# Input stage of a hybrid attention and convolution layer: meta tokens on ScalarE, position-table products moved to the start

## Chip, core and metric

The kernel runs on one core of a Trainium2 chip. The engines of a core work side by side, each through its own queue in order: TensorE (PE, with its weight loads shown apart as PEld), VectorE (DVE), ScalarE (ACT), GpSimd (POOL) and SyncE (SP), which here only issues loads and stores. ScalarE can issue them too, from its own queue. The metric is the device time of one execution, in microseconds; lower is better.

## The reference, cut to what matters

```python
h = concatenate([meta, x], axis=1)          # 16 meta rows ahead of 1024 rows of x
h = layer_norm(h, in_ln_g, in_ln_b)
z = h @ w_in + b_in                         # q | k | v | convolution input | gates
a = swa_sink_attention(q, k, v, sinks, rel_bias)   # window 128, relative bias by position
...
mixed = sigmoid(g_attn) * (a @ w_attn_proj) + sigmoid(g_conv) * (conv_branch @ w_conv_proj)
h = layer_norm(alpha * h + mixed @ w_out)
f = (gelu(g) * u) @ ffn_w_down              # u, g: up product and 3-tap convolution
return layer_norm(alpha * h + f)[:, 16:]
```

All is float32. The model width is 1024, there are 8 query heads of 64, and the relative bias comes from a table of 32 buckets by 8 heads. The kernel gets a prepared table of 33 rows: 564 columns that say which bucket each distance falls in, and 8 columns with the bias of each bucket. The product of the two parts gives the bias of every distance for every head.

## The kernel before

The layer is one long program, and PE's work through it is dense. The change touches the input stage, the first 25 us or so, and one place at 65 to 77 us.

The rows of x are loaded as eight tiles of 128 rows (`load_x`, L201), the meta rows twice into 32 rows of one tile `xm` (L198), all on SyncE's queue. Each load carries a rank: inside `with rank(p)` the instruction gets priority p, and instructions of a queue are put in the order of their priorities as far as their inputs allow. `load` issues on SyncE, `store` on ScalarE. The first three weight tiles (K, V and the first query tile) are filled with the ranks at L327.

For each group of rows, `stat` (L431) computes mean and variance on VectorE, `table` (L461) the reciprocal root of the variance on ScalarE, `newton` (L466) one Newton step and the shift -mean/std on VectorE in four small instructions, and `norm` (L475) the normed rows in two halves of 512 columns, on VectorE or ScalarE. `turns` (L492) transposes the normed rows on PE in 128-column pieces, `scaled` (L505) applies gain and bias on ScalarE, and `z_first` (L546) makes the first products: for the group of the first 272 rows directly in float32, later with split high and low parts (`high`, `low`, `whigh`, `wlow`). `dv`, `ac` and `pe` tie the instructions of VectorE, ScalarE and PE in this part into one written order each (`in_order`, L413): the list from L574 on is that order.

At its start PE runs 20 products of a constant tile with itself (L575) whose result is not used; each shows as two instructions. At the end of the input part (L663 to L669) stand the two products of the position table (400 and 164 columns, tile `ps_v`), each with a copy to `vrow` on VectorE, and a store of `vrow` to memory (`v1d`). They are tied behind the last first-stage product on PE and the last instruction of the written VectorE order.

Bank tags of PSUM: `mm` has three buffers for the first products, `o` one, `s` and `t` two each.

Of the kernel before, what the change touches and what calls it, by code (L numbers as in the profile page):

```python
# [23 lines left out]
F = mybir.dt.float32  # L24
R = mybir.dt.float32r
AF = mybir.ActivationFunctionType
# [3 lines left out]
P = 128  # L30
D = 1024
KC = D // P
NMETA = 16
# [5 lines left out]
NH = 8  # L39
# [36 lines left out]
RK_TURN, RK_SPLIT, RK_EVAC, RK_START, RK_QKV, RK_RESID, RK_ATT = 450, 500, 600, 1000, 10000, 20000, 30000  # L76
# [3 lines left out]
J_BAND, J_META, J_META0, J_METAQ, J_LEN = 0, 384, 400, 544, 564  # L80
# [32 lines left out]
def tile_hybrid_layer(  # L113
# [3 lines left out]
    nc = tc.nc  # L117
# [5 lines left out]
    def load(o, i):  # L123
        return nc.sync.dma_start(out=o, in_=i)

    def store(o, i):

        return nc.scalar.dma_start(out=o, in_=i)
# [47 lines left out]
    pat = ps_stack.enter_context(tc.tile_pool(name="pat", bufs=1, space=PSUM, reuse_waits="tile"))  # L176
# [3 lines left out]
    start = ExitStack()  # L180
    sp = start.enter_context(tc.tile_pool(name="start", bufs=1, side="right", reuse_waits="tile"))
# [10 lines left out]
    xm = sp.tile([P, D], F, name="xm")  # L192
    with rank(0):
        nc.gpsimd.memset(xm[32:64], 0.0)
        nc.gpsimd.memset(xm[64:96], 0.0)
    with rank(5):
        for i in range(2):
            load(xm[i * NMETA:(i + 1) * NMETA], meta_tokens)  # L198
    xt = []

    def load_x(j):  # L201
# [17 lines left out]

    tab = sp.tile([P, J_LEN + NH], F, name="tab")  # L220
    with rank(0):
        nc.gpsimd.memset(tab, 0.0)
    with rank(25):
        load(tab[:33], table_in)

    def bcol(m):
        return colA[:, m:m + 1]
# [94 lines left out]
    def weights(shape, fill):  # L322
        fills[0] += 1
        n = fills[0]
        own = n == 3
        raw = OB[:, 0:D].rearrange("p (k c) -> p k c", k=KC) if own else wraw(shape)
        with rank({1: 14, 2: 13, 3: 16, 4: 23}.get(n, RK_SPLIT)):  # L327
            last_fill.append(fill(raw))
        hi, lo = chunks(sp.tile([P, W_LEN], R, name="w3") if own else wsp())
        if n <= 3:  # L330
            return hi, lo, raw
        with rank(RK_SPLIT):
            last_split.append(split(raw, hi, lo))
            if n == 7:
                after(last_split[-1], cin_done[-1])
        return hi, lo
# [91 lines left out]
    def src_of(j):  # L428
        return (xt[j], P) if j >= 0 else (xm[:2 * NMETA], 2 * NMETA)

    def stat(t, *js):  # L431

        J = len(tokens[t])
        if t not in norms:
            norms[t] = [sp.tile([P, J, 2], F, name=f"mv{t}")] + [sp.tile([P, J], F, name=f"{n}{t}") for n in "trm"]
        for j in js:
            x_, n = src_of(j)
            st_ = small.tile([P, 2, 6], F, name="st")
            for i in range(2):
                dv(V.bn_stats(st_[:n, i], x_[:, i * 512:(i + 1) * 512]))  # L440
            dv(V.bn_aggr(norms[t][0][:n, tokens[t].index(j)], st_[:n].rearrange("p a b -> p (a b)")))

    def scales():
        dv(V.tensor_scalar(qb, colA[:, 0:4], HD ** -0.5, None, OP.mult))
        dv(V.tensor_scalar(colA[:, 10:30], colA[:, 10:30], 0.5, None, OP.mult))
        dv(V.tensor_scalar(nsink, sink, -1.0, None, OP.mult))

    half_st = {}

    def half_stat(t, j, i):  # L450

# [9 lines left out]
    def table(t):  # L461
        mv, t_, r_, m_ = norms[t]
        n = src_of(tokens[t][0])[1]
        ac(nc.scalar.activation(r_[:n], mv[:n, :, 1], AF.Abs_reciprocal_sqrt, bias=eps[:n], scale=1.0))

    def newton(t):  # L466
        n = src_of(tokens[t][0])[1]
        mv, t_, r_, m_ = (x_[:n] for x_ in norms[t])
        stt = V.scalar_tensor_tensor
        dv(stt(t_, mv[:, :, 1], EPS, r_, OP.add, OP.mult))  # L470
        dv(stt(t_, t_, -0.5, r_, OP.mult, OP.mult))
        dv(stt(r_, t_, 1.5, r_, OP.add, OP.mult))
        dv(stt(m_, mv[:, :, 0], -1.0, r_, OP.mult, OP.mult))

    def norm(t, j, on_dve):  # L475
        x_, n = src_of(j)
        i = tokens[t].index(j)
        mv, t_, r_, m_ = norms[t]
        xns[j] = sp.tile([P, D], F, name="xn", tag="xn", bufs=4) if j >= 0 else xm
        to = xns[j] if j >= 0 else xm[96:]  # L480
        for a in range(0, D, 512):
            if on_dve:
                dv(V.tensor_scalar(to[:, a:a + 512], x_[:, a:a + 512], r_[:n, i:i + 1], m_[:n, i:i + 1], OP.mult, OP.add))
            else:
                ac(nc.scalar.activation(to[:, a:a + 512], x_[:, a:a + 512], AF.Identity, bias=m_[:n, i:i + 1],
                                        scale=r_[:n, i:i + 1]))
        later.append((x_, mv[:n, i, 0:1], r_[:n, i:i + 1], n, j))

    GT = [(-1, 0, 1), (2, 3, 4), (5, 6, 7)]
    turned, tms = {}, {}  # L490
# [1 line left out]
    def turns(g, *ks):  # L492
        n = len(GT[g])
        c = HG[g][1] - HG[g][0]
        at = {}
        for k in ks:
            at[k] = pat.tile([P, 512], F, name="ps_h0", tag="st"[k % 2], bufs=2)
            turned[g, k] = at[k][:, n * P - c:n * P]
        for tiles in (GT[g][:2], GT[g][2:]):
            for k in ks:  # L500
                for j in tiles:
                    i = GT[g].index(j)
                    pe(nc.tensor.transpose(at[k][:, i * P:(i + 1) * P], xns[j][:, k * P:(k + 1) * P], ident))
# [29 lines left out]
    def whigh(i):  # L533
        ac(nc.scalar.copy(first[i][0], first[i][2]))
# [36 lines left out]

    tc.cur_priority = RK_START
    warm = pat.tile([P, 512], F, name="ps_w", tag="o")
    for i in range(20):  # L574
        pe(nc.tensor.matmul(warm[:, :P], ones, ones, start=True, stop=True))  # L575
    stat(0, -1)
    table(0)
    stat(1, 0)
    newton(0)
    norm(0, -1, False)  # L580
    stat(1, 1)
    table(1)
    newton(1)
    norm(1, 0, True)
    norm(1, 1, False)
    scales()
    turns(0, 0, 1, 2, 3)
    stat(2, 2)
    scaled(0, 0)
# [8 lines left out]
    evac(0, 0)  # L598
    stat(2, 3)
    stat(2, 4)  # L600
    whigh(1)
    table(2)
    z_first(0, (1,), *range(8), raw=True)
    evac(0, 1)
    newton(2)
# [55 lines left out]
    first_nm = dv_done[-1]  # L661

    tc.cur_priority = RK_RESID + 1000  # L663
    vrow = sp.tile([P, J_LEN + 104], F, name="vrow")[:NH, :J_LEN]
    for a, b in ((0, 400), (400, J_LEN)):
        ps = pat.tile([P, 512], F, name="ps_v", tag="o" if a == 0 else "t", bufs=1 if a == 0 else 2)
        after(nc.tensor.matmul(ps[:NH, :b - a], tab[:, J_LEN:], tab[:, a:b], start=True, stop=True), pe_done[-1])
        after(nc.vector.tensor_copy(vrow[:, a:b], ps[:NH, :b - a]), first_nm)
    load(v1d, vrow)  # L669

    tc.cur_priority = RK_QKV + 3000
# [1176 lines left out]
```

## Time and profile before

| | us |
|---|---|
| three runs | 1264.09, 1262.23, 1264.21 (median 1264.09) |
| the profiled execution, its own time | 1263.24 |
| its span in the trace | 1261.5 |

A row of a view names start and duration, engine, line, operation, the tile written and the tiles read, and in brackets the idle time before it and what ended it. PE's busy time counts overlapping instructions once; a full column of it does not say that each product ran at its fastest.

### The profile page before, as it was taken

Reading aid. Unit: us, or ns where it says so; the run is one execution under the profiler, and the core shown is the slowest. Engines: PE = TensorE matmul, PEld = TensorE weight load, DVE = VectorE, ACT = ScalarE, POOL = GpSimd, SP = SyncE. Lnnn points to the kernel's source line nnn. Section 1 sums busy time; section 2 is a strip of 40 time slices with the busy share of each in tenths; the row PEclk is TensorE's granted clock in tenths of the full one; section 3 lists DMA queues with packets and bytes.
Section 4 is the critical chain, followed back from the end, with each engine's and each line's share of the span. In section 5 each row is a group of like instructions: output and inputs, shape, how many; then the busy total and the mean of one; then the engine's idle time right before and its main releaser. Section 6 shows DMA issues by size and latency. Waiting matters only on the chain.

```text
span 1261.5 us, 23038 instructions
## 1 busy us (share of the span) xinstructions
PE 1247.8 (99%) x9186; PEld 1181.3 (94%) x9186; DVE 1076.5 (85%) x1858; ACT 595.0 (47%) x1100; POOL 8.0 (1%) x9
## 2 busy tenths in 40 slices
PE   8999999999999999999999999999999999999997
PEld 7999999999999999788999999999999998888886
DVE  7888999999978677448999999998989977996697
ACT  7532345655474233335665555554455544445330
POOL 0000000001000000000000000000000000000000
PEclk9999999999999999999999999999999999999999
DMA  6375543332256564222245546453454567998712
GB/s 254 105 256 145 170 120 97 106 93 85 72 155 169 164 166 124 84 85 82 68 157 196 196 171 216 160 209 135 157 205 165 192 225 252 392 353 329 271 63 84
DMA packets 98701, 212.19 MB, mean 168 GB/s; under 512 B 11411, under 2 KB 38611, under 8 KB 98338
## 3 DMA queue, kind: packets, MB, share of 16 engines
q1 hardware_dynamic: 84474, 199.64, 47.3%
q10 hardware_dynamic: 14120, 11.08, 2.8%
q8 instruction: 72, 1.18, 0.4%
q14 instruction: 35, 0.29, 0.1%
HBM read 150.29 MB, written 62.70 MB: 169 GB/s over the span
## 4 chain that ended last, share of the span: by engine, by line
PE 96%; DVE 2%; ACT 1%; DMA 0%; issue 0%; SPq 0%; DVEq 0%; ACTq 0%
PE px L1549 15%; PE py L1549 10%; PE ps_x L1694 9%; PE ps_z L342 8%; PE ps_z L345 8%; PE ps_z L346 8%; PE ps_z L1694 7%; PE pw L1549 5%; PE pz L1549 5%; PE ps_p L346 2%; PE ps_p L345 2%; PE ps_p L342 2%; PE ps_w L346 2%; PE ps_w L342 2%; PE ps_w L345 2%; PE ps_z L560 2%
## 5 line engine op out<-in xcount | busy, mean ns | idle before, releaser
L342 PE MATMUL ps_z<-RHO,w 128*128 128x256 f32 (+2 forms) x864 | 243.4, 282 | 0.0
L345 PE MATMUL ps_z<-RHO,w 128*128 128x256 f32 (+2 forms) x864 | 242.2, 280 | 0.0
L346 PE MATMUL ps_z<-RHC,w 128*128 128x256 f32 (+2 forms) x864 | 242.2, 280 | 0.0
L342 PEld LDWEIGHTS ps_z<-RHO,w 128*128 128x128 f32 x864 | 162.5, 188 | 1.2 <-ACT FA L709 0.7
L345 PEld LDWEIGHTS ps_z<-RHO,w 128*128 128x128 f32 x864 | 162.5, 188 | 0.5
L346 PEld LDWEIGHTS ps_z<-RHC,w 128*128 128x128 f32 x864 | 162.7, 188 | 0.2
L729 DVE SCALAR_TENSOR_TENSOR FA<-cin,cdw,FA 128x1026 f32<-128x1026 f32 x120 | 154.4, 1297 | 0.7
L1371 DVE TENSOR_TENSOR RHO<-wr,RHO 128x512 fp32r<-128x512 f32 x94 | 64.2, 691 | 7.9 <-ACT RHO L1370 7.9
L304 ACT CAST w<-wr 128x1024 fp32r<-128x1024 f32 x37 | 38.8, 1048 | 63.9 <-PE ps_z L346 45.0
L1370 ACT CAST RHO<-wr 128x512 fp32r<-128x512 f32 x94 | 56.8, 620 | 24.0 <-DVE wr L1388 11.8
L1388 DVE TENSOR_TENSOR wr<-wr 128x512 f32<-128x512 f32 x88 | 60.9, 692 | 0.1
L738 ACT ACTIVATE FA<-ps_z,colr 128x258 f32<-128x258 f32 (+1 forms) x64 | 30.1, 472 | 59.8 <-PE ps_z L346 48.9
L307 DVE TENSOR_TENSOR w<-wr,w 128x1024 fp32r<-128x1024 f32 x37 | 45.1, 1218 | 9.6 <-ACT w L304 9.4
L1561 ACT COPY FA<-px 128x514 f32<-128x514 f32 (+2 forms) x23 | 13.2, 573 | 76.8 <-PE px L1549 76.8
L1371 DVE TENSOR_TENSOR w<-wr,w 128x512 fp32r<-128x512 f32 x60 | 40.9, 691 | 4.8 <-ACT w L1370 4.7
L1549 PE MATMUL px<-OA,RHO 128*128 128x258 f32 x324 | 43.2, 282 | 0.0
L1476 ACT ACTIVATE FA<-OB,coll 128x512 f32<-128x512 f32 x44 | 35.9, 816 | 14.9 <-DVE OB L1557 14.9
L1370 ACT CAST w<-wr 128x512 fp32r<-128x512 f32 x60 | 36.3, 618 | 12.7 <-DMA wr<-in_w_up_dram 5.7
L1561 ACT COPY OB<-px 128x514 f32<-128x514 f32 (+2 forms) x46 | 26.1, 568 | 33.1 <-PE px L1549 33.0
L1549 PE MATMUL px<-OC,RHO 128*128 128x256 f32 x324 | 41.5, 277 | 0.0
L1549 PE MATMUL px<-RHC,RHO 128*128 128x258 f32 (+1 forms) x312 | 41.1, 281 | 0.0
L1549 PEld LDWEIGHTS px<-OA,RHO 128*128 128x128 f32 x324 | 40.5, 189 | 0.2 <-ACT OB L1561 0.2
(451 smaller groups left out, 3302.7 us busy)
## 6 DMA issues: line engine op xcount, KB each, us to landing
wr<-in_w_up_dram SPq DMA_DIRECT2D x44, 512.0 KB, 3.6
wr<-in_w_z_dram SPq DMA_DIRECT2D x29, 512.0 KB, 4.3
OB<-in_w_down_dram SPq DMA_DIRECT2D x24, 512.0 KB, 4.9
fd<-FA SPq DMA_DIRECT2D x44, 256.0 KB, 2.0
FA<-sd SPq DMA_DIRECT2D x15, 512.0 KB, 8.7
qt<-qd SPq DMA_DIRECT2D x28, 256.0 KB, 4.5
OB<-td SPq DMA_DIRECT2D x14, 512.0 KB, 10.0
sgd<-FA ACTq DMA_DIRECT2D x48, 128.0 KB, 3.0
```

Of the source, the lines that this page charges most:

```text
L304: ins = nc.scalar.copy(hi, raw)
L307: return nc.vector.tensor_tensor(lo, raw, f32(hi), OP.subtract)
L342: ins = nc.tensor.matmul(ps, al, bh, start=i == 0, stop=False)
L345: nc.tensor.matmul(ps, ah, bh, start=False, stop=False)
L346: last = nc.tensor.matmul(ps, ah, bl, start=False, stop=i == n - 1)
L729: nc.vector.scalar_tensor_tensor(acc[c], cin[:, j:j + U], wc, acc[c], OP.mult, OP.add)
L1370: nc.scalar.copy(hi, src)
L1371: ins = nc.vector.tensor_tensor(lo, src, f32(hi), OP.subtract)
L1388: ins = nc.vector.tensor_tensor(*x)
L1549: ins = nc.tensor.matmul(o, x[:, ks], bmat(sub, q, hl, k), start=first and k + j == 0, stop=k == 3 and j == 2, skip_group_check=not first)
L1561: copied.append(nc.scalar.copy(*x))
L1694: nc.tensor.matmul(banks[i], l[:, ts], r[:, ws], start=first and a and x + k == 0, stop=z and x == len(ops) - 1 and k == 2, skip_group_che ...
```

## The change

- The meta rows are loaded by ScalarE's queue with rank -1, ahead of all else there.
- The position table is cleared by VectorE instead of GpSimd, and loaded by ScalarE's queue with rank 1 instead of SyncE's with rank 25.
- The first three weight tiles have ranks 13, 16 and 19 instead of 14, 13 and 16.
- The idle products are 16 instead of 20, and both products of the table follow them directly on PE. The 164-column one takes an `mm` bank and is copied to `vrow` behind `scales()`; the 400-column one keeps the `o` bank until its copy at the old place.
- The Newton step of the meta rows runs on ScalarE, in seven small instructions (`newton_act`), and their norm is cut into its two halves, the second behind the reciprocal root of x0 and x1.
- The reciprocal root of the second group stands before, not behind, the split of the second weight tile.

```diff
-    with rank(5):
+    with rank(-1):
         for i in range(2):
-            load(xm[i * NMETA:(i + 1) * NMETA], meta_tokens)
+            store(xm[i * NMETA:(i + 1) * NMETA], meta_tokens)
...
     with rank(0):
-        nc.gpsimd.memset(tab, 0.0)
-    with rank(25):
-        load(tab[:33], table_in)
+        nc.vector.memset(tab, 0.0)
+    with rank(1):
+        store(tab[:33], table_in)
...
-        with rank({1: 14, 2: 13, 3: 16, 4: 23}.get(n, RK_SPLIT)):
+        with rank({1: 13, 2: 16, 3: 19, 4: 23}.get(n, RK_SPLIT)):
...
+    c15 = sp.tile([P, 1], F, name="c15")
+    nc.vector.memset(c15, 1.5)
...
+    def newton_act(t):
+        n = src_of(tokens[t][0])[1]
+        mv, t_, r_, m_ = (x_[:n] for x_ in norms[t])
+        act = lambda *x, **y: ac(nc.scalar.activation(*x, AF.Identity, **y))
+        act(m_, mv[:, :, 0], scale=-1.0)
+        act(t_, mv[:, :, 1], bias=eps[:n], scale=1.0)
+        for i in range(2):
+            act(t_, t_, scale=r_)
+        act(t_, t_, bias=c15[:n], scale=-0.5)
+        act(t_, t_, scale=r_)
+        act(m_, m_, scale=t_)
+        norms[t][1:3] = norms[t][2:0:-1]
...
-    for i in range(20):
+    for i in range(16):
         pe(nc.tensor.matmul(warm[:, :P], ones, ones, start=True, stop=True))
+    ps_v = []
+    vrow = sp.tile([P, J_LEN + 104], F, name="vrow")[:NH, :J_LEN]
+    for a, b in ((0, 400), (400, J_LEN)):
+        ps = pat.tile([P, 512], F, name="ps_v", tag="o" if a == 0 else "mm", bufs=1 if a == 0 else 3)
+        pe(nc.tensor.matmul(ps[:NH, :b - a], tab[:, J_LEN:], tab[:, a:b], start=True, stop=True))
+        ps_v.append((a, b, ps))
     stat(0, -1)
     table(0)
+    newton_act(0)
+    norm(0, -1, False, (0,))
     stat(1, 0)
-    newton(0)
-    norm(0, -1, False)
     stat(1, 1)
     table(1)
+    norm(0, -1, False, (512,))
     newton(1)
     norm(1, 0, True)
     norm(1, 1, False)
     scales()
+    dv(V.tensor_copy(vrow[:, 400:], ps_v[1][2][:NH, :J_LEN - 400]))
     turns(0, 0, 1, 2, 3)
...
+    table(2)
     whigh(1)
-    table(2)
...
-    vrow = sp.tile([P, J_LEN + 104], F, name="vrow")[:NH, :J_LEN]
-    for a, b in ((0, 400), (400, J_LEN)):
-        ps = pat.tile([P, 512], F, name="ps_v", tag="o" if a == 0 else "t", bufs=1 if a == 0 else 2)
-        after(nc.tensor.matmul(ps[:NH, :b - a], tab[:, J_LEN:], tab[:, a:b], start=True, stop=True), pe_done[-1])
-        after(nc.vector.tensor_copy(vrow[:, a:b], ps[:NH, :b - a]), first_nm)
+    after(nc.vector.tensor_copy(vrow[:, 0:400], ps_v[0][2][:NH, :400]), first_nm)
     load(v1d, vrow)
```

More of the change, by code (lines that the diff above doesn't have):

```diff
@@ L473, in newton, with norm @@
         dv(stt(m_, mv[:, :, 0], -1.0, r_, OP.mult, OP.mult))
-    def norm(t, j, on_dve):
+    def newton_act(t):
[10 more added lines that the diff above has]
+        norms[t][1:3] = norms[t][2:0:-1]
+    def norm(t, j, on_dve, halves=(0, 512)):
         x_, n = src_of(j)
@@ L478, in norm @@
         mv, t_, r_, m_ = norms[t]
-        xns[j] = sp.tile([P, D], F, name="xn", tag="xn", bufs=4) if j >= 0 else xm
+        if halves[0] == 0:
+            xns[j] = sp.tile([P, D], F, name="xn", tag="xn", bufs=4) if j >= 0 else xm
         to = xns[j] if j >= 0 else xm[96:]
-        for a in range(0, D, 512):
+        for a in halves:
             if on_dve:
@@ L486, in norm @@
                                         scale=r_[:n, i:i + 1]))
-        later.append((x_, mv[:n, i, 0:1], r_[:n, i:i + 1], n, j))
+        if halves[-1]:
+            later.append((x_, mv[:n, i, 0:1], r_[:n, i:i + 1], n, j))
     GT = [(-1, 0, 1), (2, 3, 4), (5, 6, 7)]
```

## The prediction

> **What bounds the kernel now.** I read the page first: the engines' totals and the chain that ended last, then the busy time by stretches.
>
> ```profile
> span 1261.5 us, 23038 instructions
> PE 1247.8 (99%) x9186; PEld 1181.3 (94%) x9186; DVE 1076.5 (85%) x1858; ACT 595.0 (47%) x1100; POOL 8.0 (1%) x9
> PE 96%; DVE 2%; ACT 1%; DMA 0%; issue 0%; SPq 0%; DVEq 0%; ACTq 0%
> 17.10:160.00 142.90, 142.65 (x1134) 139.61 (x1132) 128.47 (x192) 61.13 (x116) 0.00 (x0) 1.00 0.57 170
> 160.00:340.00 180.00, 179.67 (x1466) 176.10 (x1465) 177.30 (x377) 97.31 (x263) 5.29 (x2) 1.00 0.34 93
> ```
>
> TensorE sets the end. The columns of the last two rows are the stretch, its length, then the busy time of PE, PEld, DVE, ACT and POOL, the granted clock, the DMA share and GB/s. From 17.10 us on PE has no pause worth naming (0.25 us in 143), so whatever brings that point forward, and whatever PE no longer executes after it, comes off the end. One reserve against this: between 160 and 340 us VectorE is busy 177.3 of 180 us, so it could bind there as well.
>
> The profiled execution took 1263.24 us, 1.74 more than its span; the sum below starts from it. It lies 0.85 under the median of the shown runs, 1264.09.
>
> **The input stage, as the order of events.** The next view is the timeline of all engines, start and duration in us.
>
> ```profile
> 0.73 1.28 ACT L187 ACT_TABLE_LOAD   x1 [0.73 <-PEq L1837]
> 0.74 0.86 SPq L124 DMA_DIRECT2D xm<-in_meta_tokens_dram  x2
> 1.08 6.58 PE L575 MATMUL ps_w<-ones 128*128 128x128 f32 x40 [1.08 <-DVE ones L241]
> 1.64 0.90 SPq L124 DMA_DIRECT2D x<-in_x_dram  x2
> 1.73 0.57 POOL L222 MEMSET tab<- 128x572 f32 x1
> 2.03 0.20 ACT L187 ACTIVATE nsink<-eps 128x1 f32<-128x1 f32 x1
> 3.45 1.27 DVE L440 BATCH_NORM_STATS2 st<-xm 32x6 f32<-32x512 f32 x2 [2.41 <-DMA xm<-in_meta_tokens_dram]
> 4.99 0.29 ACT L464 ACTIVATE r<-mv,eps 32x1 f32<-32x1 f32 x1 [2.76 <-DVE mv L441]
> 5.40 1.29 DVE L440 BATCH_NORM_STATS2 st<-x 128x6 f32<-128x512 f32 x2 [0.44 <-DMA x<-in_x_dram]
> 7.42 1.27 DVE L440 BATCH_NORM_STATS2 st<-x 128x6 f32<-128x512 f32 x2
> 7.53 1.51 ACT L485 ACTIVATE xm<-xm,m,r 32x512 f32<-32x512 f32 x2 [2.25 <-DVE m L473]
> 8.72 0.21 DVE L441 BATCH_NORM_AGGREGATE mv<-st 128x2 f32<-128x12 f32 x1
> 9.07 0.29 ACT L464 ACTIVATE r<-mv,eps 128x2 f32<-128x2 f32 x1
> 10.18 1.00 DVE L483 TENSOR_SCALAR xn<-x,r,m 128x512 f32<-128x512 f32 x2
> 10.78 0.33 PE L503 MATMUL ps_h<-coll,xn 128*128 128x128 f32 x1 [2.04 <-DVE xn L483]
> ```
>
> PE's real work waits for a chain on VectorE: statistics of the meta rows (taken up by ScalarE at 4.99), of x0 (from 5.40, after 0.44 us of waiting for its load), the meta rows' Newton step, then x1 (7.42 to 8.93), reciprocal root, Newton, norm, and the transposes at 10.78. x1 takes 1.51 us of VectorE; x0 to x1 is 7.42 - 5.40 = 2.02, so the meta Newton step stands in the chain with 0.51.
>
> **Loads and Newton step.** Two things leave the chain. The two meta loads leave SyncE's queue, so x0 is issued at 0.74 instead of 1.64, 0.90 earlier; every later load moves up too. ScalarE issues them at the same 0.74, ahead of its table load, so the meta statistics keep 3.45. If x0 lands 0.9 earlier, at about 4.5, it is there before VectorE is done with the meta rows, and the 0.44 goes. The Newton step goes to ScalarE: the 0.51 goes. Together 0.95.
>
> ScalarE pays seven small instructions. Bounds from rows: 0.20 (nsink) to 0.29 (the root) each, 1.4 to 2.0 us. From 5.28 they end at 6.7 to 7.3, and the first half of the meta norm (1.51 / 2) at 7.4 to 8.1. The root for x0 and x1 is wanted at 8.93 + 0.14 - 0.95 = 8.12, so they are just covered; the second half norm stands behind that root, beside VectorE's Newton step. Were this cover gone, everything over 8.1 would be paid one to one. Ends: 0.95 if all holds, -0.3 if the table load (1.28) came ahead of the meta loads (VectorE then 1.28 late, less the 0.95). I take **0.9**, since each margin is positive but thin. The transposes then start at about 9.88.
>
> The Trainium skill, "DMA: Bandwidth & Descriptors", section "Issuing engines are not separate DMA queues", speaks against more: loads of several engines share 16 DMA engines, and a second issuer saves only issue time. That is the 0.90 us of the SyncE row; if bytes and not issue time set x0's landing, the sum would lose the 0.44 at most.
>
> The clear of the table moves from GpSimd (0.57) to VectorE ahead of the ones tile: PE starts its idle products at about 1.66 instead of 1.08. 32 instead of 40 instructions at the mean 6.58 / 40 = 0.165 last 5.3 us, to 6.9; both table products (1.14, below) end near 8.1, before 9.88. One vrow copy moves into VectorE's pause before x2; SyncE's moved weights (ranks 13, 16, 19) trade places with x2 to x4, which now come earlier; the weights they pass are used only after 17 us. These I cost at nothing; a weight over 2 us late would show as a PE pause there.
>
> **The clock.** The busy time by stretches that match the clock's steps (same columns as above), and PE's timeline.
>
> ```profile
> 8.40:11.81 3.41, 1.33 (x10) 1.17 (x11) 2.38 (x11) 2.46 (x4) 0.00 (x0) 1.00 1.02 412
> 11.81:15.22 3.41, 3.32 (x12) 2.23 (x11) 2.84 (x7) 2.57 (x5) 0.00 (x0) 0.50 1.02 416
> 612.56:615.97 3.41, 2.43 (x21) 2.42 (x21) 2.43 (x5) 3.41 (x9) 0.00 (x0) 1.00 0.82 222
> 615.97:619.39 3.42, 3.42 (x30) 3.30 (x28) 3.38 (x6) 3.42 (x8) 0.00 (x0) 1.00 0.44 144
> 12.54 1.27 PE L557 MATMUL ps_z<-FA,wr 128*128 128x272 f32 x2
> 14.25 1.11 PE L557 MATMUL ps_z<-FA,wr 128*128 128x272 f32 x2
> 15.53 0.62 PE L557 MATMUL ps_z<-FA,wr 128*128 128x272 f32 x2
> 16.31 0.62 PE L557 MATMUL ps_z<-FA,wr 128*128 128x272 f32 x2
> ```
>
> PE was busy 1.33 of 3.41 us (39%), and in the next 3.41 us the granted clock was 0.50. At 612.56 a stretch with 2.43 (71%) was followed by no drop. The price: the rounds of transposes and first products begin at 12.54, 14.25, 15.53, 16.31 and 17.10; at half clock a round takes 1.71 and 1.28, at full clock 0.78. Four at 0.785 are 3.14 instead of 4.56: **1.42** if the drop goes, 0 if it stays. With transposes 0.9 earlier the same stretch holds 1.33 + 0.9 = 2.23 (65%), or 1.93 (57%) if the lone meta transpose falls before it. Both are nearer to 71% than to 39%, so I take 1.42, with doubt.
>
> The Trainium skill, "TensorE: Matmul & The Clock Gate", section "What's actually happening", lets the clock fall after an idle window of about 3.4 us, in windows that run freely. Here it fell with no pause over 2.04 us in the rows, so the trace disagrees with that strict reading; by it the term would be 0. Free-running windows would let the term change from run to run.
>
> **The table products.** PE's timeline where they stood:
>
> ```profile
> 64.87 0.28 PE L345 MATMUL ps_z<-RHO,w 128*128 128x256 f32 x1
> 64.98 0.28 PE L346 MATMUL ps_z<-RHC,w 128*128 128x256 f32 x1
> 65.19 0.84 PE L667 MATMUL ps_v<-tab 128*8 128x400 f32 x2
> 65.96 0.38 PE L342 MATMUL ps_z<-RHO,w 128*128 128x256 f32 x1
> ...
> 71.69 0.29 PE L346 MATMUL ps_z<-RHC,w 128*128 128x272 f32 x1
> 71.91 0.44 PE L667 MATMUL ps_v<-tab 128*8 128x164 f32 x2
> 72.28 0.39 PE L342 MATMUL ps_z<-RHO,w 128*128 128x256 f32 x1
> ```
>
> Start to start they hold PE 0.77 and 0.37, 1.14 together, in a stretch without a pause. From the product before to the one behind it is 0.98 and 0.59, where an ordinary step is 0.11 and 0.13: 0.87 + 0.46 = **1.33** with the changeover. At the start they stand where PE waits for VectorE anyway, so they cost nothing there if the table has landed.
>
> **Sum:** 0.9 + 1.42 + 1.33 = 3.65; 1263.24 - 3.65 = 1259.6 us.
>
> **The rivals.**
>
> *The clock falls all the same* (chance 0.20). For it: the boundary between 39% and 71% is not known, and the idle products end only a little later than before. Then 2.23 is left: 1261.0.
>
> *The gain is lost between 160 and 340 us* (0.17). For it: VectorE is 98.5% busy there, and the order of instructions is set at build time for all engines. If its work there begins at the same time whatever PE does, the 3.65 turns into PE pauses: about 1263.2, no change. Against: VectorE has 14 us of pauses before 160 (142.90 - 128.47), so its dense stretch begins when PE delivers.
>
> *The table comes late* (0.18). PE takes its queue in order, so every transpose waits behind the table products. The load is issued by ScalarE after two meta issues (0.86), the table load (1.28) and nsink (0.20), at about 3.2. The DMA issues show what landing can take; the columns are count, KB each and median us to landing:
>
> ```profile
> xm<-in_meta_tokens_dram SPq DMA_DIRECT2D x2, 64.0 KB, 2.2
> x<-in_x_dram SPq DMA_DIRECT2D x8, 512.0 KB, 9.0
> kd<-FA ACTq DMA_DIRECT2D x1, 136.0 KB, 2.3
> ```
>
> If it goes like the last ACT row, it lands at 5.5, in time. If it shares the fate of the x loads (9.0), it lands at 12.2; PE has then paused since 6.9, the products run at half clock (2.3), and the transposes start at 14.5 instead of 10.78, 3.7 late. With the four rounds slow as before and 1.33 saved later, that is 2.4 slower: 1265.6; at 11 us to landing 1267.6. It decides from a landing 6.8 us after issue: 3.2 + 6.8 + 2.3 = 12.3 is 10.78 plus the 1.33 saved, rounded up. Against it: the table is 33 rows of 572 numbers (75 KB) on a queue with nothing but the meta loads before it.
>
> **How the numbers follow.** The forecast has 0.45, the others as given. 0.2% is 2.5 us, about what a measurement of this kernel can tell from no change. Against 1264.09 the forecast and the clock rival lie beyond it (under 1261.56): 0.65, less 0.05 for a forecast that falls short by a few tenths: faster 0.60. The lost gain (0.17), that share and the mild end of a late table (0.03) are 0.25 for same. The rest of the late table, 0.15, is slower. The ends of the chain and product terms (0.95 and 1.33, -0.3 and 1.14) put the forecast alone between 1259.5 and 1261.0. Below that the range goes to 1258.0, since the fastest run before, 1262.23, is 1.0 under the profiled one and the changeover may cost a few tenths more than its rows show. With the rivals it runs to 1265.0, which leaves out the worse part of the late table.
>
> **What would show it.** Right: x0's statistics directly behind the meta rows' at about 4.98; transposes of x0 near 9.9; no half-clock stretch before 20 us and rounds of 0.78 throughout; the 24 products that began at 17.10 begin near 14.8; no table product at 65 and 72. Wrong: PE waiting for the table's load; ScalarE reaching the second root after 8.3; a half-clock stretch behind the transposes; or a start that is 2 us ahead at 17 us and level again at 340.

## The result and the profile after

| | median us | lowest to highest | ratio to before, 95% interval |
|---|---|---|---|
| kernel before, the 9 runs beside it | 1263.02 | 1262.09 to 1264.21 | |
| changed kernel, 9 runs | 1266.64 | 1265.96 to 1267.48 | 1.0030 [1.0021, 1.0038] |

The forecast was 1259.6. The changed kernel is 3.6 us slower, and the highest time of the range, 1265.0, is 1.6 under it. The profiled execution took 1266.68 us. From its page, the engines' totals and the chain that ended last:

```profile
span 1264.7 us, 23024 instructions
PE 1248.0 (99%) x9178; PEld 1182.3 (93%) x9178; DVE 1074.4 (85%) x1856; ACT 596.4 (47%) x1107; POOL 7.4 (1%) x8
PE 88%; DVE 7%; DMA 2%; ACT 1%; issue 1%; DVEq 0%; ACTq 0%; SPq 0%
```

PE has eight instructions less and the same busy time; in the chain, VectorE went from 2% to 7% and loads from 0% to 2%. The timeline of the start:

```profile
0.75 0.89 ACTq L128 DMA_DIRECT2D xm<-in_meta_tokens_dram  x2
0.75 0.86 SPq L124 DMA_DIRECT2D x<-in_x_dram  x2
6.75 1.27 DVE L440 BATCH_NORM_STATS2 st<-xm 32x6 f32<-32x512 f32 x2 [5.09 <-DMA xm<-in_meta_tokens_dram]
8.18 1.22 DVE L440 BATCH_NORM_STATS2 st<-x 128x6 f32<-128x512 f32 x2
8.26 1.12 PE L597 MATMUL ps_v<-tab 128*8 128x400 f32 x4
8.49 0.18 ACT L480 ACTIVATE m<-mv 32x1 f32<-32x1 f32 x1
9.56 1.23 DVE L440 BATCH_NORM_STATS2 st<-x 128x6 f32<-128x512 f32 x2
10.20 0.29 ACT L480 ACTIVATE m<-m,t 32x1 f32<-32x1 f32 x1
10.52 0.81 ACT L501 ACTIVATE xm<-xm,m,t 32x512 f32<-32x512 f32 x1
10.83 0.21 DVE L441 BATCH_NORM_AGGREGATE mv<-st 128x2 f32<-128x12 f32 x1
11.36 0.30 ACT L466 ACTIVATE r<-mv,eps 128x2 f32<-128x2 f32 x1
13.07 0.33 PE L520 MATMUL ps_h<-coll,xn 128*128 128x128 f32 x1 [1.34 <-DVE xn L499]
14.83 1.27 PE L574 MATMUL ps_z<-FA,wr 128*128 128x272 f32 x2
16.54 1.11 PE L574 MATMUL ps_z<-FA,wr 128*128 128x272 f32 x2
```

Both queues issue at 0.75, as forecast. The meta statistics, though, wait 5.09 us for the load and begin at 6.75 instead of 3.45. The x0 statistics follow at 8.18 without a wait and x1 ends at 10.83 + 0.21 = 11.04. The first transpose of x0 is at 13.07 instead of 10.78, 2.29 late. The table's products, at 8.26, delay nothing. The busy time by stretches (start and end; length; busy time of PE, PEld, DVE, ACT, POOL; granted clock, DMA share, GB/s), the first three cut where the record of the granted clock, which goes in steps of 3.41 us, cuts them in this execution:

```profile
7.33:10.74 3.41, 1.99 (x12) 0.96 (x10) 3.34 (x8) 2.26 (x9) 0.00 (x0) 1.00 1.03 411
10.74:14.15 3.41, 1.38 (x11) 1.22 (x12) 2.58 (x13) 3.22 (x5) 0.00 (x0) 1.00 1.03 411
14.15:17.57 3.42, 3.28 (x12) 2.20 (x10) 3.32 (x9) 2.56 (x5) 0.00 (x0) 0.50 1.02 407
77.00:100.00 23.00, 22.72 (x192) 22.52 (x191) 17.91 (x22) 5.98 (x10) 0.00 (x0) 1.00 0.88 272
100.00:160.00 60.00, 59.06 (x522) 58.78 (x521) 55.56 (x79) 19.54 (x40) 0.00 (x0) 1.00 0.55 141
```

The last two stretches in the kernel before:

```profile
77.00:100.00 23.00, 23.00 (x200) 23.00 (x199) 18.87 (x22) 5.98 (x10) 0.00 (x0) 1.00 0.79 235
100.00:160.00 60.00, 59.87 (x532) 59.67 (x530) 55.49 (x83) 20.03 (x41) 0.00 (x0) 1.00 0.56 152
```

The clock falls to 0.50 here too, at 14.15 instead of 11.81, and again behind a stretch in which PE was busy for only 40% (1.38 of 3.41). PE stands still for 0.28 + 0.94 us between 77 and 160, where it stood still for 0.13 in all before.

For where the time went, the two traces are laid side by side: the offset is the start of an instruction in one kernel less the start of the same instruction (n-th with the same operation, tiles and shape) in the kernel before, in the two profiled executions. For PE, changed kernel against before:

```
at us     11    17    64    74    90   340   606   609   end
offset +2.29 +2.31 +2.06 +0.50 +1.40 +2.62 +2.60 +3.60 +3.23
```

It begins 2.29 late, wins 1.56 where the table's products no longer run (64 to 74), loses 2.12 by 340 and another 1.00 at 607. The spans differ by the last column; 0.2 more lies outside them.

### The profile page after: what moved, and what is told of

It is laid out like the page before. It is cut to its first block, busy times and chain, and to the rows that moved or that the text cites. A ratio compares the mean times of both kernels' runs of the same rounds, so it can differ in the third digit from the quotient of the medians.

```text
span 1264.7 us, 23024 instructions
## 1 busy us (share of the span) xinstructions
PE 1248.0 (99%) x9178; PEld 1182.3 (93%) x9178; DVE 1074.4 (85%) x1856; ACT 596.4 (47%) x1107; POOL 7.4 (1%) x8
## 4 chain that ended last, share of the span: by engine, by line
PE 88%; DVE 7%; DMA 2%; ACT 1%; issue 1%; DVEq 0%; ACTq 0%; SPq 0%
PE px L1570 15%; PE py L1570 10%; PE ps_x L1715 9%; PE ps_z L1715 7%; PE ps_z L342 6%; PE ps_z L345 6%; PE ps_z L346 6%; PE pz L1570 5%; PE pw L1570 5%; DVE FA L750 3%; PE ps_p L345 2%; PE ps_p L346 2%; PE ps_p L342 2%; PE ps_w L346 2%; PE ps_w L342 2%; PE ps_w L345 2%
```

## Experiments

All times are medians, each with its ratio to runs of the kernel before on the same chip beside it.

| run | median us | ratio, 95% interval | offset at 17 | 64 | 74 | 340 | 606 | 609 | end |
|---|---|---|---|---|---|---|---|---|---|
| e1_meta_sp | 1261.86 | 0.9993 [0.9984, 1.0001] | -1.66 | -1.91 | -3.48 | -2.14 | -2.14 | -1.14 | -1.50 |
| e2_meta_act_alone | 1266.24 | 1.0024 [1.0015, 1.0034] | +2.62 | +2.32 | +2.32 | +2.24 | +2.23 | +2.23 | +2.07 |
| e3_products_alone | 1262.33 | 0.9996 [0.9987, 1.0005] | -1.15 | -1.48 | -3.05 | -2.08 | -2.09 | -1.04 | -1.28 |
| e4_products_late | 1266.78 | 1.0030 [1.0018, 1.0042] | +3.80 | +3.46 | +3.47 | +4.39 | +3.53 | +3.53 | +3.78 |
| e5_one_meta_load | 1268.55 | 1.0046 [1.0032, 1.0060] | +5.27 | +5.03 | +3.47 | +4.09 | +4.09 | +5.07 | +4.80 |
| e6_newton_dve | 1266.42 | 1.0027 [1.0016, 1.0038] | +3.35 | +3.19 | +1.62 | +2.63 | +2.63 | +3.61 | +3.26 |
| e8_bank_t | 1261.87 | 0.9993 [0.9984, 1.0002] | -1.38 | -1.73 | -3.30 | -2.71 | -2.71 | -2.72 | -2.82 |
| e9_no_products | 1262.53 | 0.9997 [0.9988, 1.0006] | -1.11 | -1.14 | -2.71 | -2.51 | -2.53 | -2.53 | -2.60 |
| e10_split_meta | 1261.75 | 0.9993 [0.9984, 1.0002] | -1.28 | -1.73 | -3.30 | -2.31 | -2.30 | -2.30 | -2.42 |
| e11_bank_alone | 1264.33 | 1.0012 [1.0003, 1.0020] | -0.11 | +1.93 | +1.21 | +1.22 | +1.21 | +1.21 | +1.06 |
| e12_pause_filled | 1263.85 | 1.0005 [0.9996, 1.0014] | -1.20 | -1.02 | -1.02 | -1.40 | -1.41 | -1.41 | +0.00 |
| e13_bank_t_fill | 1261.70 | 0.9992 [0.9984, 1.0001] | -0.19 | -0.53 | -2.09 | -1.52 | -1.53 | -1.53 | -1.52 |
| e14_after_bank_t | 1266.47 | 1.0028 [1.0018, 1.0039] | +3.53 | +3.18 | +1.61 | +3.50 | +3.50 | +3.50 | +3.90 |
| e15_order_before | 1266.02 | 1.0027 [1.0017, 1.0036] | +2.21 | +1.97 | +0.40 | +1.35 | +1.51 | +2.55 | +2.33 |
| e16_order_before_bank_t | 1265.93 | 1.0026 [1.0015, 1.0037] | +2.64 | +2.41 | +0.84 | +1.52 | +1.52 | +1.52 | +2.08 |

The offsets come from one execution each, the medians from 4 to 11, so the two can differ by about 1 us.

### The meta loads (e1, e2, e10, e5)

**Back on SyncE, in the changed kernel:**

```diff
-    with rank(-1):
+    with rank(5):
         for i in range(2):
-            store(xm[i * NMETA:(i + 1) * NMETA], meta_tokens)
+            load(xm[i * NMETA:(i + 1) * NMETA], meta_tokens)
```

> The changed kernel with the two meta loads back on SyncE's queue, rank 5, all else as changed. Theory Q (loads are served in the order of issue over both queues: the second meta load stood behind x0 and x1, and VectorE waited for it until 6.75 us): meta statistics start near 3.5, those of x0 near 5.4, first transpose of x0 near 10.3 instead of 13.07, time 1262 to 1263. Theory S (ScalarE's seven small instructions and the table's load are what is late): first transpose of x0 not before 11, time 1264 or more.

Its timeline:

```profile
0.75 0.86 SPq L124 DMA_DIRECT2D xm<-in_meta_tokens_dram  x2
3.44 1.27 DVE L440 BATCH_NORM_STATS2 st<-xm 32x6 f32<-32x512 f32 x2 [1.78 <-DMA xm<-in_meta_tokens_dram]
5.76 1.29 DVE L440 BATCH_NORM_STATS2 st<-x 128x6 f32<-128x512 f32 x2 [0.81 <-DMA x<-in_x_dram]
7.20 1.23 DVE L440 BATCH_NORM_STATS2 st<-x 128x6 f32<-128x512 f32 x2
12.19 0.72 PE L574 MATMUL ps_z<-FA,wr 128*128 128x272 f32 x2 [0.34 <-ACT FA L526]
13.08 0.62 PE L574 MATMUL ps_z<-FA,wr 128*128 128x272 f32 x2
```

This one part undone takes 4.8 us off the median. The meta rows are there at 3.44 again. x0 to x1 is 7.20 - 5.76 = 1.44 instead of 2.02, so the Newton step is out of VectorE's chain, as forecast; x0 itself waits 0.81 instead of 0.44, with the table's load now beside it.

**Alone on ScalarE, in the kernel before** (the same four lines the other way round):

> The kernel before with only the two meta loads moved to ScalarE's queue, rank -1. Theory Q: meta statistics start after 6 us, first transpose of x0 near 13.5, time 1266 to 1267. Theory S: meta statistics start near 3.5, time within 1 us of before (1263).

```profile
0.74 0.89 ACTq L128 DMA_DIRECT2D xm<-in_meta_tokens_dram  x2
6.68 1.28 DVE L440 BATCH_NORM_STATS2 st<-xm 32x6 f32<-32x512 f32 x2 [5.64 <-DMA xm<-in_meta_tokens_dram]
8.12 1.22 DVE L440 BATCH_NORM_STATS2 st<-x 128x6 f32<-128x512 f32 x2
```

Nothing but the queue of two loads of 64 KB is edited; SyncE then issues x0 and x1 0.9 earlier. PE executes the same instructions in the same order as before, and VectorE all but one, at 220 us. The meta statistics begin at 6.68, and the kernel is 3.1 us slower (1266.24 beside 1263.10): this move by itself is most of the 3.6 of the whole change. The parts don't simply add up. With the meta loads on SyncE the rest of the change is worth about -1.2 (e1, not told from no change), with them on ScalarE nothing that can be told (1266.64 beside 1266.24).

**One on each queue,** in e8 (below):

```diff
+    with rank(-1):
+        store(xm[0:NMETA], meta_tokens)
     with rank(5):
-        for i in range(2):
-            load(xm[i * NMETA:(i + 1) * NMETA], meta_tokens)
+        load(xm[NMETA:2 * NMETA], meta_tokens)
```

> The kernel with the 164-column product in a bank of t (1261.87 in an earlier run), with one of the two meta loads issued by ScalarE ahead of all else, the other by SyncE as before; x0 is then SyncE's second load instead of its third. Theory Q (a load lands in the order of its issue among all loads, and the second meta load was late only because x0 and x1 were issued between): both meta loads are issued ahead of x0, so the meta statistics start at 3.4 to 3.8 and x0's at 5.0 to 5.4, the first transpose of x0 at 9.9 to 10.3. Rival S (a load on ScalarE's queue is late by itself beside SyncE's): the meta load on ScalarE lands at 4.8 as the first one did in the changed kernel, the meta statistics start there, the first transpose at 11.1 to 11.6; time 1 above, 1262.8.

```profile
0.75 0.43 ACTq L128 DMA_DIRECT2D xm<-in_meta_tokens_dram  x1
0.75 0.39 SPq L124 DMA_DIRECT2D xm<-in_meta_tokens_dram  x1
1.20 0.88 SPq L124 DMA_DIRECT2D x<-in_x_dram  x2
3.42 1.27 DVE L441 BATCH_NORM_STATS2 st<-xm 32x6 f32<-32x512 f32 x2 [1.76 <-DMA xm<-in_meta_tokens_dram]
4.85 1.28 DVE L441 BATCH_NORM_STATS2 st<-x 128x6 f32<-128x512 f32 x2
7.17 1.29 DVE L441 BATCH_NORM_STATS2 st<-x 128x6 f32<-128x512 f32 x2 [0.79 <-DMA x<-in_x_dram]
```

ScalarE's load of 64 KB is there by 3.42: its queue is not slow in itself. In the changed kernel the other load issued at 0.75 was x0 with 512 KB, and the second meta load came beside x1. By the trace they landed at 4.76 and 6.65, x0 between them at 5.86; here, with both small loads issued ahead of all large ones, they are there by 3.03 and 3.39. x0 no longer waits (4.85), and now x1 does, 0.79, so the first transpose comes no sooner than in e1: offset -0.33, in e1 -0.36. When a load lands thus hangs on what was issued ahead of it or at the same moment, on either queue. Theory Q's strict order of issue goes too far: in the changed kernel nothing was issued ahead of the first meta load, and it still landed 1.4 later than here. That agrees with the Trainium skill, "DMA: Bandwidth & Descriptors", section "Issuing engines are not separate DMA queues": loads of all engines run on the same 16 DMA engines and interleave.

**Both copies in one load of ScalarE, in the changed kernel:**

```diff
-        for i in range(2):
-            store(xm[i * NMETA:(i + 1) * NMETA], meta_tokens)
+        store(xm[:2 * NMETA], dram(meta_tokens, 0, [[0, 2], [D, NMETA], [1, D]]))
```

> The changed kernel with both copies of the meta rows in one load of 128 KB, still on ScalarE's queue at 0.75. Theory Q (loads of both queues are served in the order of issue, and the second meta load stood behind x0 and x1 because it was issued after them; it landed at 6.64): the one load is issued before x1 and partly before x0, so the meta statistics start between 4.8 (the landing of the first meta load) and 5.9 (that of x0), 0.9 to 2.0 ahead of 6.75, and the first transpose of x0 stands at 11.1 to 12.2 instead of 13.07. Time 0.5 to 2 us under the changed kernel (1264.6 to 1266.1 beside 1266.6). Rival S (ScalarE's queue is slow in itself, whatever is issued when): the statistics stay at 6.75 and the time at 1266.6.

Neither: it was the slowest of all. The timeline, and the busy time of two stretches:

```profile
9.46 1.27 DVE L439 BATCH_NORM_STATS2 st<-xm 32x6 f32<-32x512 f32 x2 [7.80 <-DMA xm<-in_meta_tokens_dram]
8.00:9.00 1.00, 0.00 (x0) 0.00 (x0) 0.00 (x0) 0.00 (x0) 0.00 (x0) 1.00 0.98 298
9.00:10.00 1.00, 0.16 (x1) 0.12 (x2) 0.54 (x1) 0.00 (x0) 0.00 (x0) 1.00 0.37 141
```

The load's packets of 4 KB run in the trace as two trains, 0.16 us from packet to packet at first, from 3.57 on, then between the packets of x and the weights until past 8; from 9 to 10 the DMA share is down to 0.37. Two trains fit a load that went to two of the 16 engines. The Trainium skill states such a rule, "DMA: Bandwidth & Descriptors", section "Why a DMA increments its semaphore by 16 and not by 1": the number of engines is the largest up to 16 that divides the outermost sizes of both patterns, and here one of them is 2. The kernel says nothing about order of issue; it tested another thing than was meant.

### The Newton step (e6)

```diff
-    newton_act(0)
-    norm(0, -1, False, (0,))
     stat(1, 0)
+    newton(0)
+    norm(0, -1, False, (0,))
```

> The changed kernel with the meta rows' Newton step back on VectorE, at its old place between x0 and x1. The prediction's theory (the step on ScalarE takes 0.51 off the chain): x1's statistics start 0.5 later, transposes at 13.5, time 0.5 above the changed kernel, 1267.1. Rival N (ScalarE's seven instructions, 2.0 us in the trace, hold up the root for x0 and x1 by as much as VectorE saves): the root stands 0.2 to 0.5 later than 11.36, the transposes at 13.1 to 13.4, time within 0.3 of the changed kernel, 1266.4 to 1266.9.

x1's statistics end later than in the changed kernel and ScalarE is free at once, but its root for x0 and x1 comes at 11.58 instead of 11.36 and the transposes at 13.29 instead of 13.07: 0.22, inside what the rival gave. Counted from the x0 statistics, which began 0.11 earlier in e6 (8.07 against 8.18), it is 0.33, so the move keeps 0.33 of its 0.51. ScalarE's seven instructions run from 8.49 to 10.49 in the changed kernel, 2.00 us, the upper of the bounds taken for them; with the half norm behind them (10.52 to 11.33) they hold the root, due at 11.04 + 0.14 = 11.18, until 11.36. That is the missing 0.18. The time (1266.42) can't be told from the changed kernel's, and e6 has its instructions in another order from about 120 us on.

### The products of the table (e3, e4, e9)

**The table's part alone** in the kernel before, with the change's products and copies:

```diff
-        nc.gpsimd.memset(tab, 0.0)
-    with rank(25):
-        load(tab[:33], table_in)
+        nc.vector.memset(tab, 0.0)
+    with rank(1):
+        store(tab[:33], table_in)
...
-    for i in range(20):
+    for i in range(16):
...
```

> The kernel before with only the table's part of the change: cleared by VectorE, loaded by ScalarE's queue with rank 1, 16 idle products and both table products behind them, one vrow copy early. If PE sets the end at 65 to 150 us, the removed products are worth 1.3 to 1.7 us: 1261.3 to 1261.7. If VectorE sets it there (theory V: from 17 us on VectorE works without pause, and what PE saves turns into waits for cin and for the attention blocks), 0 to 0.9 us: 1262.1 to 1263.

**Products and copies at their old place** in the changed kernel:

```diff
-    ps_v = []
...
-        ps_v.append((a, b, ps))
...
+        after(nc.tensor.matmul(ps[:NH, :b - a], tab[:, J_LEN:], tab[:, a:b], start=True, stop=True), pe_done[-1])
+        after(nc.vector.tensor_copy(vrow[:, a:b], ps[:NH, :b - a]), first_nm)
```

> The changed kernel with the two table products and both vrow copies back at their old place (the table's early load stays). Theory V: VectorE sets the pace, only its copy counts: 1266.6 to 1267.5. If PE sets it: 1.3 to 1.7 us slower than the changed kernel, 1268 or more.

**No products** in the kernel before (the relative bias is then not computed):

```diff
-        ps = pat.tile([P, 512], F, name="ps_v", tag="o" if a == 0 else "t", bufs=1 if a == 0 else 2)
-        after(nc.tensor.matmul(ps[:NH, :b - a], tab[:, J_LEN:], tab[:, a:b], start=True, stop=True), pe_done[-1])
-        after(nc.vector.tensor_copy(vrow[:, a:b], ps[:NH, :b - a]), first_nm)
+        after(nc.vector.tensor_copy(vrow[:, a:b], tab[:NH, a:b]), first_nm)
```

> The kernel before, with both products of the position table left out and the two copies to vrow reading the table's own rows instead, so the relative bias is not computed. All else is as before, the start too. The prediction's theory (PE has no pause from 17 us on, so what it no longer executes at 65 and 72 us comes off the end): 1.33 less at the end, 1261.7 beside 1263.0. Rival V (VectorE sets the pace from 50 to 340 us): PE is 1.2 to 1.7 ahead at 78 us, gives it back as pauses before VectorE's results by 160 us, and the end is within 0.4 of the kernel before, 1262.6 to 1263.0.

In every kernel without them at 65 and 72 us PE wins 1.56 or 1.57 between 64 and 74 us. By 90 us 0.5 to 0.9 of it is given back (0.48 in e9, 0.90 in the changed kernel). A part of that is a pause at one row, here that of e9 and then that of the changed kernel, where PE waits for VectorE to finish a tile; the rest does not show as a pause:

```profile
75.49 0.39 PE L342 MATMUL ps_z<-RHO,w 128*128 128x256 f32 x1 [0.19 <-DVE cin L715]
```

```profile
78.79 0.38 PE L342 MATMUL ps_z<-RHO,w 128*128 128x256 f32 x1 [0.28 <-DVE cin L738]
```

From 17 to 606 us e9 wins 2.53 - 1.11 = 1.42 in the trace, near the 1.33 of the forecast. Its median is only 0.5 lower, with an interval that takes in no change, and lies nearer to rival V's forecast. How much of the 1.42 reaches the time is therefore open. e3's median, 1262.33, lies where theory V had put it: its trace wins 1.57 by 74, loses 0.97 of it by 340 and another 1.05 at 607 (see below). e4's, 1266.78, does too, but e4 against the changed kernel is no pure test: its clock fell for longer (+3.80 at 17, against +2.31), and its instructions stand in another order, see below.

### The granted clock (e12, e13)

24 idle products instead of 20 in the kernel before (e12), and 18 instead of 16 in e8 (e13):

```diff
-    for i in range(20):
+    for i in range(24):
```

> The kernel before with 24 idle products instead of 20, so that PE's pause ahead of the transposes at 10.78 starts at 9.0 to 10.2 instead of 7.7; nothing else. The prediction's clock term (with PE busy for more of that stretch the granted clock does not fall, worth 1.42): rounds of 0.78 throughout, the 24 products at 17.10 start 1.1 to 1.4 earlier, the time 0.4 to 1.1 under the kernel before (of whose runs about a third have the higher mean clock already), 1262.0 to 1262.6. Rival: the fall does not hang on this pause: rounds of 1.71 and 1.28 as before, 1263.0.

> The kernel with the 164-column product in a bank of t and the meta loads on SyncE's queue (1261.87), with 18 idle products instead of 16, so that the table's products end at about 9.9, just ahead of the transposes at 10.34. If the clock falls in some executions because of the pause of 0.9 that is left there: a higher mean clock in all runs and 1261.4. If two more products delay the transposes, or the fall does not hang on this pause: 1261.9 to 1262.3.

Two stretches of the profiled execution of e12, then two of e13, each cut where the clock's record cuts them in that execution (to 0.04 us):

```profile
6.80:10.20 3.40, 2.71 (x24) 2.47 (x23) 2.66 (x12) 1.81 (x3) 0.00 (x0) 1.00 0.99 370
10.20:13.60 3.40, 2.37 (x17) 2.01 (x18) 2.67 (x9) 3.10 (x6) 0.00 (x0) 1.00 1.03 419
```

```profile
8.15:11.56 3.41, 1.86 (x13) 1.15 (x12) 2.87 (x13) 2.62 (x4) 0.00 (x0) 1.00 1.02 399
11.56:14.98 3.42, 3.39 (x12) 2.35 (x11) 3.07 (x9) 2.56 (x5) 0.00 (x0) 0.50 1.03 418
```

PE busy for 80% of the first stretch: no fall, and the first 17 us are 1.20 shorter. At 55% (1.86 of 3.41) it fell, and most of that is lost again (-0.19 at 17). Over all the traces of this case a fall followed the stretches with 9 to 40% and two with 47 and 55%, and none followed any with 58% or more at full clock; three with 43 to 46% went by without a fall, so the busy time of PE alone does not draw the line. The fall lasted one stretch of 3.41 us where PE was busy for 96% or more of it, and two where it was 33 to 90% (e4, e5, e6, e14, e16); in e4 and e14 the offset grows by 1.2 between 11 and 17. The idle products lasted only 5.72 us in this execution of e13, and up to 6.51 (changed kernel) where there are four fewer instructions, so a fixed number does not fill the pause each time.

The fall comes and goes between executions of one kernel. The traces have one execution of each, but they tell how to read the runs: all six without a fall have a mean granted clock of 0.998 or more, all eleven with one 0.997 or less. Of 33 runs of the kernel before, 22 had a mean granted clock of 0.997 or less and took 1263.32 on average, 11 had 0.998 or more and took 1261.98. In the other three sets of its runs beside the experiments the difference is 0.85, 1.26 and 1.36, and of all 100 runs 35 had the higher clock. With the table's products in the pause and the meta rows in time, 37 of 55 runs had 0.998 or more (e1, e3, e8, e10, e13); of the changed kernel's nine, none. The lower time forecast for e12 did not come: it has the higher clock in 7 of 11 runs, and loses what it won between 800 and 1100 us (offset -1.11 to +0.01), with its instructions in another order; whether that order is the cause was not tested. e13's median, 1261.70, with the higher clock in 6 of 11 runs, is neither of its two forecasts.

### The loss at 607 us, and the order of the program (e8, e11, e14 to e16)

In the changed kernel and then in e1, the first product of the up stage waits for VectorE to empty a bank:

```profile
610.67 1.53 PE L1570 MATMUL px<-OC,RHO 128*128 128x256 f32 x11 [0.79 <-DVE OB L1325]
```

```profile
605.93 1.65 PE L1570 MATMUL px<-OC,RHO 128*128 128x256 f32 x12 [0.78 <-DVE OB L1325]
```

The 164-column product had moved from a bank of `t` to one of `mm`, which turns the rotation of three banks by one. e8 is e1 with the bank of `t`; PE and VectorE keep the order of e1:

```diff
-        ps = pat.tile([P, 512], F, name="ps_v", tag="o" if a == 0 else "mm", bufs=1 if a == 0 else 3)
+        ps = pat.tile([P, 512], F, name="ps_v", tag="o" if a == 0 else "t", bufs=1 if a == 0 else 2)
```

> The changed kernel with the meta loads back on SyncE's queue (1261.86 in an earlier run), and the 164-column product in a bank of t, as before, instead of one of mm. Theory B (one more tile in mm shifts the rotation of its three banks, so that at 607 us the up stage's first products get a bank that VectorE has not emptied yet, which costs 0.9): the offset against the kernel before stays at -2.1 from 600 to the end instead of shrinking to -1.3, and the time is 0.7 to 1.0 lower, about 1261.0, ratio 0.9985. Rival: the loss at 607 comes from the earlier arrival at that stage and not from the bank: the time stays at 1261.9.

The offset stays where it was at 606 (-2.71 to -2.72), where e1 lost 1.00. The medians, 1261.86 and 1261.87, don't show it: the time came out as the rival had it. The other way round, the bank alone changed in the kernel before:

> The kernel before, at its old place the 164-column product takes a bank of mm instead of t; nothing else. Theory B (the shifted rotation of mm costs about 0.9 at 607 us): the offset to the kernel before is 0 up to 600 and +0.9 to +1.0 from 609 on, the time 0.8 to 1.0 higher, 1263.9. Rival: the loss at 607 comes with an earlier start alone: no offset, 1263.0.

It did more than that. The two products now stand at 56 us, and 1.2 us are lost by 74; and PE's instructions from about 120 us on stand in another order. A planner orders the whole program at build time, so one edit can move instructions far from it. In the traces PE keeps the order of the kernel before, but for the products at the start and those of the table, in e1, e2, e3, e5, e8, e9 and e13 (in e10 one instruction is moved as well). The changed kernel has another order from about 120 us on, and e11 has, from 90 us on, the changed kernel's on PE and VectorE; e4, e6 and e12 have others. On VectorE the changed kernel's order leaves the old one at the taps of the convolution, about 96 us. The changed kernel with 14 idle products in place of 16 has the order of the kernel before. So e14 is the changed kernel with the bank of `t`, as in the diff of e8, in its own order; e15 is the changed kernel with this one line, and e16 has both edits:

```diff
-    for i in range(16):
+    for i in range(14):
```

> The changed kernel with the 164-column product in a bank of t instead of one of mm; the order of the instructions on PE and VectorE is that of the changed kernel. Theory B (the bank costs about 1.0 at 607 us): the offset to the kernel before stays where it is at 606 us instead of rising by 1.0, and the time is 0.7 to 1.0 under the changed kernel, 1265.7. Rival: the loss at 607 is only moved on and the end stays, 1266.6.

> The changed kernel with 14 idle products instead of 16. With 14, the planner that orders the program at build time puts the instructions of PE and VectorE behind the input stage (from about 105 us on) in the order of the kernel before; with 16 it puts them in another (2225 lines of difference on PE instead of 102). Theory O (that other order is where the saving of the table's products went between 90 and 600 us): the first transpose stays near 13.1, the offset is +2.3 at 17, +0.5 at 74, +1.0 to +1.4 at 90 and no more than that up to 600, the time 1 to 1.5 under the changed kernel, 1265.1 to 1265.6. Rival V (VectorE, which starts 2.2 later than before, sets the pace there): the offset climbs to +2.1 to +2.6 by 340 all the same, time 1266.2 to 1266.6.

> The changed kernel with both: 14 idle products (order of the kernel before) and the 164-column product in a bank of t. Theories O and B together: 1264.2 to 1264.8, so that only the late start (2.3 us) less the products' saving is left. Rivals V and no bank effect: 1266.2 to 1266.6.

From e15, two stretches to hold against those of the changed kernel:

```profile
77.00:100.00 23.00, 22.71 (x195) 22.51 (x194) 17.90 (x22) 5.98 (x10) 0.00 (x0) 1.00 0.90 270
100.00:160.00 60.00, 59.64 (x528) 59.43 (x528) 56.46 (x82) 19.74 (x41) 0.00 (x0) 1.00 0.54 146
```

Up to 100 us both stand still alike (0.28 and 0.29). From 100 to 160 PE is idle 0.36 with the old order and 0.94 with the new one, and from 74 to 340 the offset grows by 0.95 and 0.68 (e15, e16) instead of 2.12 and 1.89 (changed kernel, e14). So between these traces the other order took about 1.2 us. It does not do so by itself: e11 has the same order there, and PE has no pause in it from 100 to 160, its offset +1.21 at 74 and +1.22 at 340:

```profile
100.00:160.00 60.00, 60.00 (x532) 59.97 (x531) 57.61 (x85) 19.92 (x41) 0.00 (x0) 1.00 0.54 144
```

What has to come with it, the late start or the gain at 64 to 74, no run tells. The bank is worth the 1.0 at 609 in e14 and e16 too, of which about half is lost again by 620 (+3.50 to +4.04, +1.52 to +2.12). And again it is not enough alone: e11 has the bank of `mm` and loses nothing at 607 (+1.21 before and behind it). In time, against the changed kernel, the order alone is worth 0.6 us (e15), the bank alone 0.2 (e14) and both 0.7 (e16). That is the right direction and less than theories O and B had forecast, with intervals that overlap that of the changed kernel: it isn't settled by the runs.

## Why the prediction was wrong

| term | forecast | trace |
|---|---|---|
| chain of loads and statistics up to the first transpose | -0.9 | +2.29 |
| clock, up to 17 us | -1.42 | +0.02 |
| products off PE, 64 to 74 us | -1.33 | -1.56 |
| 74 to 340 us | 0 | +2.12 |
| at 607 us | 0 | +1.00 |
| the rest | 0 | -0.64 |
| sum | -3.65 | +3.23 |

**The step that failed** is in "Loads and Newton step": "ScalarE issues them at the same 0.74, ahead of its table load, so the meta statistics keep 3.45." The time of issue was right. From it I took the time of landing, as if the 2.2 us from issue to landing of the row on SyncE belonged to the load. They belonged to its place: nothing large was ahead of it or beside it. The DMA view of the changed kernel has 4.0 us in its place:

```profile
xm<-in_meta_tokens_dram ACTq DMA_DIRECT2D x2, 64.0 KB, 4.0
```

Issued at the same moment as x0 and x1, the two landed at 4.76 and 6.65. The start moved from -0.9 to +2.29, an error of 3.2 of the 6.9 between the two sums. e2 shows it by itself, e1 undoes it, and e10 shows that the queue is not slow. The rule of the Trainium skill that I cited there was the right one; I applied it to x0 alone, as a loss of 0.44 at the most, and not to the load that was moved. The lower end of that term, -0.3, came from a table load on ScalarE and not from the DMA engines, so neither the range nor a rival held the mechanism that decided. And x0, issued 0.90 earlier, landed not at 4.5 but at 5.86 in the changed kernel, later than the 5.37 of the kernel before; where the small loads are first (e10) it is there by 4.85, and x1 is late instead.

**The clock.** The forecast counted on a stretch of 65% in place of 39%, between the same two times as in one trace of the kernel before. Those times are not fixed: the stretch ahead of the fall ended at 11.81 there, at 14.15 in the changed kernel and at 11.56 in e13. With the start 2.29 late it held 1.38 us of PE's work in the changed kernel, 40%, and the rival "the clock falls all the same" came true. The size was nearly right: 0.94 to 1.31 between 11 and 17 us in the traces without a fall, 0.85 to 1.36 between the two groups of runs of the kernel before. What was wrong is to take it as a property of the kernel: by the mean clock a third of the runs before had no fall already, and two thirds of those with the products in the pause and the meta rows in time. An estimate from the 33 and 55 runs above gives a change in the mean of (37/55 - 11/33) x 1.34 = 0.45, not 1.42. The Trainium skill's sentence on windows that run freely ("TensorE: Matmul & The Clock Gate", section "What's actually happening") was the better guide here than the single profile: in these traces the stretches are 3.41 us long and begin at another time in each.

**The products.** 1.33 was right for PE (1.56 at the place, 1.42 up to 606 in e9). "From 17.10 us on PE has no pause worth naming (0.25 us in 143), so [...] whatever PE no longer executes after it, comes off the end" was wrong in the changed kernel: e9's trace keeps nearly all of the gain (its median 0.5), the changed kernel's none of it. The reserve about VectorE came true in part, at 78 us and not between 160 and 340; the larger parts went with another order of the program and, in this trace, with a bank that was not free, each together with something that no run has singled out. Neither was in the forecast, which took the order of everything behind the input stage as fixed.

**The rest held, or cost nothing:** the Newton step on ScalarE held the root up by 0.18, as the upper bound allowed; the table's load was in time, and its rival named the wrong load, so that the measured time inside its 1265.6 to 1267.6 is chance; the 32 idle instructions took 6.51 us instead of 5.3, since a mean over 40 mixes a slow and a fast part (see the end), which PE's pause covered; the clear of the table and the moved weights cost nothing that the traces show.

## What to carry to other kernels

A load's time from issue to landing, read in a profile, holds for what was ahead of it and beside it then: before moving a small load that everything waits for to another queue, list what the other queues issue at the same moment, and let the large loads come after it. A gain measured on one profiled execution may already be there in a third of the runs, so look at the granted clock of all runs before counting it. And when a program is ordered at build time, compare the order of the instructions before comparing times: an edit of two idle products moved over two thousand lines here. Of the versions run, e13 (1261.70), e10, e1 and e8 (up to 1261.87) all keep the meta loads, or one of them, on SyncE; they are 4.8 to 4.9 us under the changed kernel and 1.1 to 1.4 under the kernel before, and against the latter each interval still touches no change.

## What was not expected of the hardware

- Two loads of 64 KB on ScalarE's queue kept VectorE until 6.7 us where the same two on SyncE's were there by 3.4, with 512 KB loads issued beside them instead of behind them.
- A load of 128 KB whose source pattern has an outermost size of 2 went out in two trains of packets (e5) and landed at about 9.4 us, issued at 0.75.
- The same 40 idle instructions took 6.29 us in e11, 6.58 in the kernel before and 7.58 in e2. In these three traces they start 0.21 us apart at first and 0.11 apart later, and the change comes where the record of the granted clock begins, at 4.39, 4.99 and 7.08: PE's part of the start has no fixed length, because that moment is another in each execution.
